# Norm factors of a decoder layer: the sum of squares as the moving operand of a constant, and a reciprocal root with one Newton step

## The chip, the cores and the metric

The kernel runs on one core of a Trainium2 chip. The metric is the device time of one execution, in microseconds (us). Engines are named as the profile names them: PE is TensorE (PEld its weight loads), DVE is VectorE, ACT is ScalarE, POOL is GpSimd, SP is SyncE, which here only issues DMAs. F32R and F32 are two types under which a float32 operand is handed to TensorE.

## What is computed

One layer of a hybrid decoder trunk over 512 tokens and a model width of D = 1024, batch 1, all in float32: a half-step SwiGLU FFN (hidden width 2816), a token mixer (RG-LRU on 512 channels beside sliding-window attention with 8 heads of 64), and a second half-step FFN. Every sub-layer has an RMS norm on its input and one on its output:

```python
def rms_norm(x, g):
    y = xf * lax.rsqrt(jnp.mean(xf * xf, axis=-1, keepdims=True) + RMS_EPS)
    return (y * g).astype(x.dtype)

x = x + 0.5 * rms_norm(swiglu(rms_norm(x, ffn1_pre_g), ffn1_w_gu, ffn1_w_down), ffn1_post_g)
y = concat([rms_norm(y_lru, g_lru_out), rms_norm(y_attn, g_attn_out)]) @ w_o     # mixer, from rms_norm(x, mix_pre_g)
x = x + rms_norm(y, mix_post_g)
x = x + 0.5 * rms_norm(swiglu(rms_norm(x, ffn2_pre_g), ffn2_w_gu, ffn2_w_down), ffn2_post_g)
```

What matters here is the norm factor, 1/sqrt(mean of squares + eps), one number for each token.

## The kernel before

**Layout.** Activations lie transposed: channels on the 128 partitions, the 512 tokens along the free dimension, so a width of 1024 is eight tiles of 128x512. The sum of squares over channels therefore runs over partitions and over tiles. The tiles' squares (ACT, line 552) are added up on DVE or POOL into one 128x512 tile, `acc`; what is left is a sum over the 128 partitions, and the factor is then needed on all partitions, as a 128x512 tile that multiplies the data.

**Matmuls.** Each float32 operand is split into a high part (F32R) and the rest, a low part, and each product is three matmuls: high by high, high by low, low by high. ACT makes a high part by copying (`act.copy`, lines 195 to 215; `x_high`, line 641), DVE or POOL the low part by subtracting it (`x_low`, line 644). Weights come from HBM through `class Weights`: `load` issues the DMA, `round` makes the high part on ACT, `fill(n)` makes both parts until n units beyond those taken are ready. A unit's low part is made by DVE, by POOL, or, for the unit marked `shared`, half by DVE and half by POOL.

**The factor before.** `InvRmsRows` makes it for all 512 tokens at once, `InvRms` for half of them (256). In `stats`, `acc` stands as weights, 128 tokens at a time, and a single column of 1/D moves past it: the means arrive with tokens on partitions, one column per block of 128 tokens (lines 569 and 608). Then follow a square root on ACT (575, 615), a reciprocal on DVE (577, 616), the split into high and low part (583, 584, 617, 618), and a multiplication of the identity matrix by the factors, which gives diagonal blocks (588, 621). In `spread`, a matmul of an all-ones matrix by these diagonals (595, 625) brings the factors to all partitions, in PSUM. In the half-width form the first half has a single plain F32 diagonal, the second a high and a low one. A full-width factor is then copied to SBUF as `R` by ACT (689), or read from PSUM (`lru`, line 1976); a half-width factor is read from PSUM by DVE in `Residual.scale`.

**Where factors are made**, in order of time: `x`, for the first norm (full width; its squares are summed by ACT, so it has no statistics matmul); `r1`, two halves, the norm behind the first FFN; `mx`, full width, before the mixer; `lru`, full width, inside it; `r2`, two halves, behind the mixer; `f2` (shown as `nf`), full width, before the second FFN. Two half-width pairs and three full-width factors thus go the whole way from `acc`. The attention's own norm and the one at the very end are made otherwise and are not touched.

**The boundary.** `boundary` joins a sub-layer to the next one, once as "a" (FFN 1 to mixer: `r1`, then `mx`) and once as "m" (mixer to FFN 2: `r2`, then `f2`). All engines run in an order written out by hand (`manual_schedule`): each executes its instructions in the order in which the code emits them, waits on semaphores, and passes nothing that waits. The last three output chunks, c = 5, 6, 7, are multiplied in two token halves, each product over n = 6 ("a") or n = 8 ("m") tiles of the contraction, three 256-column matmuls for each. The code then goes on as follows, where (k, h) is chunk k of token half h:

- first half of the three products; after each, DVE takes it out of PSUM (751 or 755), ACT squares it, DVE adds it to `acc2` (764 to 768), and `W.fill` prepares weights;
- second half: in the middle of product c = 6 the hook `stats` for half 0, and one contraction tile later `W.fill(4)`; ahead of product c = 7 `spread` of half 0 and the steps for chunks 0 and 1;
- a step for chunk k is: `scale`, DVE multiplies y by the gain and the factor in one instruction (772); `add`, the residual sum into `xT`, on DVE for even k and on POOL for odd k (776); `high`, ACT makes the high part for the next matmul (641);
- `k_high` on PE (540, 541): pass k multiplies chunk k's high part by four weight tiles, each high and low, 8 matmuls; passes 0 to 3 of half 0, then `stats` of half 1, passes 4 and 5, `spread` of half 1, passes 6 and 7, then the eight passes of half 1. Meanwhile the steps of the remaining chunks of half 0 and of all of half 1 run;
- `low` for all chunks (DVE, 644), `W.fill(2)`, the next norm's squares into its `acc` (ACT 552, DVE 681), and `k_low` on PE (547), 32 matmuls of 512 columns. The next full-width factor is asked for in the middle of the product that follows.

In "a" the weight unit that `W.fill(4)` prepares is the `shared` one (DVE and POOL, 195); in "m" its low part is made by POOL alone (215).

Of the kernel before, what the change touches and what calls it, by code (L numbers as in the profile page):

```python
# [8 lines left out]
F32 = mybir.dt.float32  # L9
F32R = mybir.dt.float32r  # L10
# [112 lines left out]
def tile_layer(ctx: ExitStack, tc: tile.TileContext, out: bass.AP, **ins: bass.AP):  # L123
# [357 lines left out]
    ones = const.tile([P, P], F32R, name="ones")  # L481
    dve.memset(ones.bitcast(F32), 1.0)
# [8 lines left out]
    mean_d = filled("mean_d", 1, 1.0 / D)  # L491
    mean_c = filled("mean_c", 1, 1.0 / C)
# [63 lines left out]

    class InvRms:


        def __init__(self, accs, mean, half, name, eps=eps):  # L560
            self.accs, self.mean, self.half, self.name, self.eps = accs, mean, half, name, eps

        def stats(self):
            self.ps = ps = bank(f"rms_{self.name}")
            self.dg = []
            for i in range(2):
                b = 2 * self.half + i
                for j, a in enumerate(self.accs):
                    pe.matmul(ps[:, i:i + 1], a[:, b * P:(b + 1) * P], self.mean, start=j == 0, stop=j == len(self.accs) - 1)
            self.invert(ps[:, :2])  # L570

        def invert(self, ms, scale=1.0):
            n = self.name
            rms = small.tile([P, 2], F32, tag="rms", name=f"rms_s{n}")
            act.activation(rms, ms, AF.Sqrt, bias=self.eps, scale=scale)
            rs = small.tile([P, 2], F32, tag="rs", name=f"rs_{n}")
            dve.reciprocal(rs, rms)
            split = self.half == 1
            factors, w = [rs], ones.bitcast(F32)
            if split:  # L580
                high = small.tile([P, NB], F32R, tag="rh4", name=f"rh4_{n}", bufs=1)[:, :2]
                low = small.tile([P, NB], F32, tag="rl4", name=f"rl4_{n}", bufs=1)[:, :2]
                dve.tensor_copy(high, rs)
                dve.tensor_sub(low, rs, high.bitcast(F32))
                factors, w = [rs, low], ones
            t = wt(f"dg_{n}", T, F32R if split else F32)
            for sl, r in zip(HALF, factors):
                dve.tensor_tensor(t[:, sl].rearrange("p (a b) -> p a b", a=2), ident.unsqueeze(1).to_broadcast([P, 2, P]),
                                  r.unsqueeze(2).to_broadcast([P, 2, P]), op=ALU.mult)
                self.dg.append((w, t[:, sl]))  # L590

        def spread(self):
            o = self.ps[:, T // 2:]
            for i, (w, d) in enumerate(self.dg):
                pe.matmul(o, w, d, start=i == 0, stop=i == len(self.dg) - 1)
            return o


    class InvRmsRows:


        def __init__(self, acc, mean, name):
            self.acc, self.mean, self.name = acc, mean, name

        def stats(self):
            self.ps = ps = bank(f"rms_{self.name}")
            for b in range(NB):
                pe.matmul(ps[:, b:b + 1], self.acc[:, b * P:(b + 1) * P], self.mean, start=True, stop=True)
            self.invert(ps[:, :NB])

        def invert(self, ms, scale=1.0):
            n = self.name
            rms, rs, low = (small.tile([P, NB], F32, tag=t, name=f"{t}_{n}", bufs=1) for t in ("rms4", "rs4", "rl4"))
            high = small.tile([P, NB], F32R, tag="rh4", name=f"rh4_{n}", bufs=1)
            act.activation(rms, ms, AF.Sqrt, bias=eps, scale=scale)
            dve.reciprocal(rs, rms)
            dve.tensor_copy(high, rs)
            dve.tensor_sub(low, rs, high.bitcast(F32))
            self.dg = [wt(f"d{i}_{n}", T, F32R) for i in "hl"]
            for d, r in zip(self.dg, (rs, low)):  # L620
                dve.tensor_tensor(v4(d), ident.unsqueeze(1).to_broadcast([P, NB, P]), r.unsqueeze(2).to_broadcast([P, NB, P]), op=ALU.mult)

        def spread(self):
            for i, d in enumerate(self.dg):
                pe.matmul(self.ps, ones, d, start=i == 0, stop=i == 1)
            return self.ps
# [31 lines left out]
    class Next:  # L658


        def __init__(self, name, pre=None, gain=None):
            self.name, self.pre = name, pre
            self.gain = gain or (lambda c: col(pre, c))
            self.t = {}
            self.xs = x_parts(name)
            self.acc = tmp.tile([P, T], F32, tag="acc", name=f"acc_n{name}", bufs=3)
            self.rms = InvRmsRows(self.acc, mean_d, f"n{name}")
            self.R = None
# [14 lines left out]
        def stats(self):  # L683
            self.rms.stats()
# [1517 lines left out]
```

## Time and profile before

| | us |
|---|---|
| median of 3 runs (lowest to highest) | 835.47 (835.04 to 835.94) |
| the profiled execution's own time | 834.93 |
| its span, first to last instruction | 833.0 |
| PE busy | 825.3 |
| DVE busy | 737.6 |
| ACT busy | 518.5 |
| POOL busy | 164.7 |
| granted TensorE clock, mean | 0.999 |

The profile is one execution. Busy is the time in which an engine had an instruction running; consecutive matmuls overlap, so what a matmul costs is read from the distance between starts. In a timeline row the first number is the start from the beginning of the span, the second the time it took, then engine, line, operation, output and inputs; "x4" is a number of merged instructions, and a bracket at the end tells how long the engine had been idle and what ended that.

### The profile page before, as it was taken

How to read it: one execution, taken by the hardware profiler on the slowest of the kernel's cores; microseconds unless marked ns; L12 is line 12 of the kernel's file. 1: busy time of each engine (PE TensorE's matmuls, PEld its weight loads, DVE VectorE, ACT ScalarE, POOL GpSimd, SP SyncE). 2: the span in 40 equal slices, each digit the busy share in tenths (PEclk: the TensorE clock that was granted, in tenths of full speed). 3: DMA queues.
4: the chain of work that ended last, by engine and by line, in shares of the span. 5: the costliest groups of instructions: out<-in, count | busy, mean ns of one | idle time of the engine just before them, and what ended most of it. 6: DMA issues, size and time to landing. Idle time of an engine off the chain costs nothing.

```text
span 833.0 us, 11751 instructions
## 1 busy us (share of the span) xinstructions
PE 825.3 (99%) x4188; PEld 700.3 (84%) x4188; DVE 737.6 (89%) x1033; ACT 518.5 (62%) x811; POOL 164.7 (20%) x187
## 2 busy tenths in 40 slices
PE   9999999999999999999999999999999999999997
PEld 8888888888888898987888899888888888888885
DVE  5989799998989978888989689998999798898996
ACT  6746656676666654546797446545757677676552
POOL 2022000140320325414531052002005023032001
PEclk9999999999999999999999999999999999999999
DMA  7376408398595897522611140567439949669742
GB/s 254 103 278 226 152 22 322 75 263 253 139 260 170 196 272 243 175 89 82 174 37 51 51 143 10 123 180 253 130 107 239 309 94 252 234 159 260 300 141 102
DMA packets 121835, 144.22 MB, mean 173 GB/s; under 512 B 24168, under 2 KB 76720, under 8 KB 121264
## 3 DMA queue, kind: packets, MB, share of 16 engines
q1 hardware_dynamic: 107280, 112.26, 42.1%
q0 software_dynamic: 13792, 30.42, 16.6%
q10 hardware_dynamic: 704, 0.79, 0.3%
q8 instruction: 33, 0.54, 0.3%
q14 instruction: 26, 0.21, 0.1%
HBM read 100.45 MB, written 39.32 MB: 168 GB/s over the span
## 4 chain that ended last, share of the span: by engine, by line
PE 98%; DVE 0%; DMA 0%; issue 0%; SPq 0%; DVEq 0%
PE ab L1026 10%; PE aa L1026 10%; PE db L1026 5%; PE da L1026 5%; PE yaa L1427 3%; PE a_first L1289 3%; PE bb L1026 3%; PE ba L1026 3%; PE ya L1427 3%; PE yda L1427 2%; PE aa L956 1%; PE yab L2042 1%; PE yab L2041 1%; PE yab L2040 1%; PE wo L1966 1%; PE gt L522 1%
## 5 line engine op out<-in xcount | busy, mean ns | idle before, releaser
L1198 POOL DMA_DIRECT2D yr_a<-stage x36 | 31.1, 1004 | 176.0 <-ACT stage L1195 153.6
L1198 POOL DMA_DIRECT2D yp_b<-stage x42 | 36.5, 1064 | 146.3 <-ACT stage L1195 119.8
L2056 POOL DMA_DIRECT2D yp_b<-stage x8 | 4.4, 547 | 64.7 <-ACT stage L2055 64.3
L745 POOL TENSOR_TENSOR acca_r<-acca_r,sq_r 128x512 f32<-128x512 f32 x6 | 9.1, 1517 | 38.2 <-ACT sq_r L552 38.1
L540 PE MATMUL an<-xh_mx,whi_xl 128*128 128x256 f32 x64 | 15.7, 285 | 0.0
L541 PE MATMUL an<-xh_mx,wlo_xl 128*128 128x256 f32 x64 | 15.5, 283 | 0.0
L2157 ACT ACTIVATE ysq<-yp 128x512 f32<-128x512 f32 (+1 forms) x8 | 4.8, 606 | 16.8 <-DVE yp L2150 16.8
L2160 POOL TENSOR_TENSOR last<-yp,grow 128x512 f32<-128x512 f32 x3 | 3.9, 1288 | 57.0 <-DVE yp L2150 57.0
L522 PE MATMUL gt<-xh_mx,whi_gt 128*128 128x512 f32 x32 | 14.2, 443 | 0.0
L1464 POOL DMA_DIRECT2D yp_a<-zy x16 | 8.7, 555 | 25.5 <-DMA rows_a<-yr_a 17.3
L498 ACT ACT_TABLE_LOAD x9 | 11.5, 1283 | 2.4 <-issue 2.3
L522 PE MATMUL pq<-xh_mx,whi_q 128*128 128x512 f32 x32 | 12.8, 399 | 0.0
L524 PE MATMUL gt<-xh_mx,wlo_gt 128*128 128x512 f32 x32 | 12.6, 394 | 0.0
L522 PE MATMUL pgb<-xh_f,whi_bg 128*128 128x512 f32 x32 | 12.6, 393 | 0.0
L523 PE MATMUL gt<-xl_mx,whi_gt 128*128 128x512 f32 x32 | 12.5, 391 | 0.0
L524 PE MATMUL pq<-xh_mx,wlo_q 128*128 128x512 f32 x32 | 12.5, 390 | 0.0
L523 PE MATMUL pq<-xl_mx,whi_q 128*128 128x512 f32 x32 | 12.5, 390 | 0.0
L524 PE MATMUL pgb<-xh_f,wlo_bg 128*128 128x512 f32 x32 | 12.5, 390 | 0.0
L522 PE MATMUL pub<-xh_f,whi_bu 128*128 128x512 f32 x32 | 12.5, 389 | 0.0
L523 PE MATMUL pub<-xl_f,whi_bu 128*128 128x512 f32 x32 | 12.5, 389 | 0.0
L523 PE MATMUL pgb<-xl_f,whi_bg 128*128 128x512 f32 x32 | 12.5, 389 | 0.0
L524 PE MATMUL pub<-xh_f,wlo_bu 128*128 128x512 f32 x32 | 12.5, 389 | 0.0
(2028 smaller groups left out, 3398.6 us busy)
## 6 DMA issues: line engine op xcount, KB each, us to landing
yp_b<-stage POOLq DMA_DIRECT2D x50, 256.0 KB, 9.1
yr_a<-stage POOLq DMA_DIRECT2D x44, 256.0 KB, 9.9
h_a<-za SPq DMA_DIRECT2D x16, 256.0 KB
h_b<-zb SPq DMA_DIRECT2D x16, 256.0 KB
hxb<-h_b SPq DMA_DIRECT2D x16, 256.0 KB
hxa<-h_a SPq DMA_DIRECT2D x6, 512.0 KB
raw_ad<-in_ffn_w_down SPq DMA_DIRECT2D x2, 1024.0 KB
xT_hbm<-xT POOLq DMA_DIRECT2D x2, 1024.0 KB, 6.1
```

The lines of the kernel that those rows point to most:

```text
L498: act.activation(dummy, eps, func)
L522: pe.matmul(ps, hi[:, k, :], xh, start=start, stop=False)
L523: pe.matmul(ps, hi[:, k, :], xl, start=False, stop=False)
L524: pe.matmul(ps, lo[:, k, :], xh, start=False, stop=stop)
L540: pe.matmul(ps[:, sl], hi[:, k, :], xh, start=k == 0 and not goes_on, stop=False, skip_group_check=True)
L541: pe.matmul(ps[:, sl], lo[:, k, :], xh, start=False, stop=False, skip_group_check=True)
L745: eng.tensor_add(acc, acc, square(part, ALL, f"{self.name}{c}"))
L1026: pe.matmul(b[tb], x[:, blk], w[:, k, :], start=first and q + k + j == 0, stop=q + k == 2 and j == 2, skip_group_check=True)
L1198: pool.dma_start(o, st, accum_op=ALU.add)
L1289: pe.matmul(banks[j][:, sl], ws[j][part][:, k, :], n1.xs[k][xpart][:, sl], start=k == 0 and part == xpart, stop=stop and k == KD - 1)
L1427: pe.matmul(o, x[:, blk], a[:, k, :], start=start and j == 0, stop=stop and j == 2, skip_group_check=True)
L1464: (pool if q % 2 else sync).dma_start(chunks[32 * q:32 * (q + 1), :, i * P:(i + 1) * P], turned[32 * i:32 * (i + 1), :, q])
```

## The change

A constant matrix of -1.0, `minus`, takes the place of `ones` and stands as weights; `acc` is now what moves, as plain F32, in one matmul of 512 or 256 columns. Its output is minus the sum of squares, on all 128 partitions at once. ACT makes an approximate factor r from it with `Abs_reciprocal_sqrt` (its scale turns the sign and divides by D, its bias adds eps) and then a scaled square of r; DVE makes one Newton step in two instructions, the first of them reading the sum from PSUM. The result r lies in SBUF. The statistics matmuls with one column, the roots, the reciprocals, the splits, the diagonals, `spread` and the copy to `R` are gone for these factors. `x` keeps its old way, with `minus` as weights and a sign turned by the copy.

In `boundary`, `stats` of half 0 is asked for one contraction tile earlier (`n // 2 - 1`). In "a", `W.fill(4)` is replaced at its place by a `round` of one unit (ACT only), and comes after the steps for chunks 0 and 1; in "m" it keeps its place. `scale` reads r, in SBUF, where it read the factor in PSUM. The function that ACT preloads is `Abs_reciprocal_sqrt` instead of `Sqrt` in two places.

```diff
-    ones = const.tile([P, P], F32R, name="ones")
-    dve.memset(ones.bitcast(F32), 1.0)
+    minus = const.tile([P, P], F32R, name="minus")
+    dve.memset(minus.bitcast(F32), -1.0)
...
+    NEWTON = {D: (eps4, -1.0 / 256, 1.0 / 16, 3.0), C: (eps, -1.0 / 512, 1.0 / 32, 1.5)}
+
     class InvRms:
-        def stats(self):
-            self.ps = ps = bank(f"rms_{self.name}")
...
-        def spread(self):
...
+        def stats(self, r, sl=slice(0, T), q=None):
+            bias, scale, root, k = NEWTON[self.n]
+            ps = bank(f"rms_{self.name}")[:, sl]
+            pe.matmul(ps, minus.bitcast(F32), self.acc[:, sl], start=True, stop=True)
+            q = wt(f"q_{self.name}")[:, sl] if q is None else q
+            act.activation(r, ps, AF.Abs_reciprocal_sqrt, bias=bias, scale=scale)
+            act.activation(q, r, AF.Square, scale=root)
+            dve.scalar_tensor_tensor(q, ps, self.n * EPS, q, op0=ALU.subtract, op1=ALU.mult)
+            dve.scalar_tensor_tensor(r, q, k, r, op0=ALU.add, op1=ALU.mult)
+            self.r = r
+
+    class InvRmsHalf(InvRms):
...
         def stats(self):
+            t = wt(f"r_{self.name}")
+            super().stats(t[:, HALF[0]], HALF[self.half], t[:, HALF[1]])
...
         def spread(self):
             if self.R is None:
-                self.R = big.tile([P, T], F32, tag="R", name=f"R_{self.name}")
-                act.copy(self.R, self.rms.spread())
+                self.R = self.rms.r
...
-        def spread_a():
-            spread(0)
-            steps((0, 1), 0, bcs[0])
+        def round_next():
+            if W.rounded == W.split:
+                W.round()
+
+        def first_steps():
+            steps((0, 1), 0, res.rms[0].r)
+            W.fill(4)
 
         n = len(xs)
-        hooks = [{}, {n // 2: res.rms[0].stats, n // 2 + 1: lambda: W.fill(4)}, {0: spread_a}]
+        hooks = [{}, {n // 2 - 1: res.rms[0].stats, n // 2 + 1: round_next if parts else lambda: W.fill(4)}, {0: first_steps}]
...
-                preload(AF.Sqrt)
+                preload(AF.Abs_reciprocal_sqrt)
...
     def spread_lru():
-        bc = lrms.spread()
+        bc = lrms.r
...
-            wo_attn([c], lrms.stats)
+            wo_attn([c], lambda: lrms.stats(wt("r_lru")))
```

More of the change, by code (lines that the diff above doesn't have):

```diff
@@ L572, in invert @@
[L572 to L590, printed above, removed]
@@ L592, in spread @@
-        def spread(self):
[L593 to L603, printed above, removed]
-        def stats(self):
[L606 to L626, printed above, removed]
@@ new lines, in __init__ @@
+        def __init__(self, acc, n, name):
+            self.acc, self.n, self.name = acc, n, name
+        def stats(self, r, sl=slice(0, T), q=None):
[8 more added lines that the diff above has]
+            self.r = r
@@ L629, in stream, with __init__ @@
+    class InvRmsHalf(InvRms):
+        def __init__(self, acc, half, name):
+            super().__init__(acc, D, name)
+            self.half = half
+        def stats(self):
+            t = wt(f"r_{self.name}")
+            super().stats(t[:, HALF[0]], HALF[self.half], t[:, HALF[1]])
     def stream():
@@ L666, in __init__ @@
             self.acc = tmp.tile([P, T], F32, tag="acc", name=f"acc_n{name}", bufs=3)
-            self.rms = InvRmsRows(self.acc, mean_d, f"n{name}")
+            self.rms = InvRms(self.acc, D, f"n{name}")
             self.R = None
@@ L730, in __init__ @@
             self.acc, self.acc2 = (tmp.tile([P, T], F32, tag="acc", name=f"acc{i}_{name}", bufs=3) for i in "ab")
-            self.rms = [InvRms([self.acc2], mean_d, h, f"{name}{h}") for h in range(2)]
+            self.rms = [InvRmsHalf(self.acc2, h, f"{name}{h}") for h in range(2)]
         def chunk(self, c, ps, part=None, eng=pool, first=None):
@@ L809, in boundary @@
                 for k in (2, 3):
-                    res.scale(k, 0, bcs[0])
+                    res.scale(k, 0, res.rms[0].r)
                 res.add(2, 0)
@@ L831, in boundary @@
         for k in (6, 7):
-            res.scale(k, 0, bcs[0])
+            res.scale(k, 0, res.rms[0].r)
         for k in (6, 7):
@@ L840, in boundary @@
         k_high(ws, banks, nxt.xs, HALF[0], range(4, 6))
-        spread(1)
         for k in (0, 1):
-            res.scale(k, 1, bcs[1])
+            res.scale(k, 1, res.rms[1].r)
             res.add(k, 1)
@@ L846, in boundary @@
         for k in range(2, KD, 2):
-            steps((k, k + 1), 1, bcs[1])
+            steps((k, k + 1), 1, res.rms[1].r)
         k_high(ws, banks, nxt.xs, HALF[0], range(6, 8))
@@ L1256, in first_lo, with stats @@
         eng.tensor_sub(lo, raw, hi.bitcast(F32))
-    class InvRmsX(InvRmsRows):
+    class InvRmsX:
         def early(self):
-            ss = small.tile([P, NB], F32, tag="ss", name=f"ss_{self.name}", bufs=1)
+            ss, rms, rs, low = (small.tile([P, NB], F32, tag=t, name=f"{t}_x", bufs=1) for t in ("ss", "rms4", "rs4", "rl4"))
+            high = small.tile([P, NB], F32R, tag="rh4", name="rh4_x", bufs=1)
             sx = ssx.rearrange("p (b h) -> p b h", h=2)
             dve.tensor_add(ss, sx[:, :, 0], sx[:, :, 1])
-            self.invert(ss, 1.0 / D)
-        def stats(self):
-            self.ps = bank(f"rms_{self.name}")
-    n1.rms = InvRmsX(None, None, "x")
+            act.activation(rms, ss, AF.Sqrt, bias=eps, scale=1.0 / D)
+            dve.reciprocal(rs, rms)
+            dve.tensor_copy(high, rs)
+            dve.tensor_sub(low, rs, high.bitcast(F32))
+            self.dg = [wt(f"d{i}_x", T, F32R) for i in "hl"]
+            for d, r in zip(self.dg, (rs, low)):
+                dve.tensor_tensor(v4(d), ident.unsqueeze(1).to_broadcast([P, NB, P]), r.unsqueeze(2).to_broadcast([P, NB, P]), op=ALU.mult)
+        def stats(self, r):
+            ps = bank("rms_x")
+            for i, d in enumerate(self.dg):
+                pe.matmul(ps, minus, d, start=i == 0, stop=i == 1)
+            act.activation(r, ps, AF.Copy, scale=-1.0)
+            self.r = r
+    n1.rms = InvRmsX()
     warm = bank("warm")
@@ L1276, in spin @@
         for i in range(n):
-            pe.matmul(warm[:, (i % 4) * P:(i % 4 + 1) * P], ones.bitcast(F32), ones.bitcast(F32), start=True, stop=True)
+            pe.matmul(warm[:, (i % 4) * P:(i % 4 + 1) * P], minus.bitcast(F32), minus.bitcast(F32), start=True, stop=True)
     spin(WARM)
@@ L1954, in tile_layer @@
     W.round()
-    preload(AF.Sqrt)
-    lrms = InvRmsRows(accl, mean_c, "lru")
+    preload(AF.Abs_reciprocal_sqrt)
+    lrms = InvRms(accl, C, "lru")
     res = Residual("r2", lambda c: col("mix_post_g", c))
```

19 lines of the change are left out of this document (3 added, 16 removed).

## The prediction

> **What bounds the kernel now.** I read the page's first part, its chain of work, and the waits of PE.
>
> ```profile
> span 833.0 us, 11751 instructions
> ...
> PE 825.3 (99%) x4188; PEld 700.3 (84%) x4188; DVE 737.6 (89%) x1033; ACT 518.5 (62%) x811; POOL 164.7 (20%) x187
> ...
> PE 98%; DVE 0%; DMA 0%; issue 0%; SPq 0%; DVEq 0%
> ```
>
> PE is busy for 825.3 of 833.0 us and is 98% of the chain that ends last. Its column of issued matmuls is the kernel's length, so the change counts in two ways only: PE work it adds or removes, and gaps it opens or closes in that column. The boundaries are where gaps can open: there PE multiplies what DVE, POOL and ACT have finished just before. One gap is already visible, in boundary "a", pass 1 of half 1:
>
> ```profile
> 349.75 0.28 PE L541 MATMUL an<-xh_mx,wlo_xl 128*128 128x256 f32 x1
> 349.96 0.39 PE L540 MATMUL an<-xh_mx,whi_xl 128*128 128x256 f32 x1
> ```
>
> Starts stand 0.12 us apart here, but 0.21 at this place. The chain that makes high parts has no reserve there, and a later factor lengthens the kernel one for one.
>
> **PE's own work.** First a half-width factor of boundary "a", half 0, then the full-width `mx`, both from PE's timeline.
>
> ```profile
> 336.31 0.50 PE L569 MATMUL rms_r<-mean_d,accb_r 128*128 128x1 f32 x4
> 336.68 0.36 PE L522 MATMUL ay<-hha,whi_ad 128*128 128x256 f32 x1
> 336.88 0.28 PE L523 MATMUL ay<-hla,whi_ad 128*128 128x256 f32 x1
> ...
> 337.71 0.28 PE L524 MATMUL ay<-hha,wlo_ad 128*128 128x256 f32 x1
> 337.92 0.67 PE L595 MATMUL rms_r<-dg_r,ones 128*128 128x256 f32 x2
> 338.24 0.47 PE L522 MATMUL ay<-hha,whi_ad 128*128 128x256 f32 x1
> 338.55 0.28 PE L523 MATMUL ay<-hla,whi_ad 128*128 128x256 f32 x1
> ```
>
> The statistics cost 0.37 (336.31 to 336.68) and 0.08 more at the next step (0.20 instead of 0.12): 0.45. From 337.71 to 338.55 there would be 0.24 without the spread; it costs 0.60, of which 0.09 is its late start (337.92, not 337.83). So a plain F32 matmul of 256 columns takes 0.51, about four steps of 0.12, and its result is complete 0.67 after its start.
>
> ```profile
> 366.77 0.95 PE L608 MATMUL rms_nmx<-mean_d,acc_nmx 128*128 128x1 f32 x8
> 367.58 0.49 PE L522 MATMUL pk<-xh_mx,whi_kv 128*128 128x512 f32 x1
> 367.91 0.40 PE L523 MATMUL pk<-xl_mx,whi_kv 128*128 128x512 f32 x1
> ...
> 370.46 0.39 PE L625 MATMUL rms_nmx<-dh_nmx,ones 128*128 128x512 f32 x1
> 370.69 0.39 PE L625 MATMUL rms_nmx<-dl_nmx,ones 128*128 128x512 f32 x1
> 370.91 0.40 PE L522 MATMUL pv<-xh_mx,whi_kv 128*128 128x512 f32 x1
> ```
>
> Full width: statistics 0.81 + 0.10 (0.33 instead of 0.23), spread 0.45, together 1.36. The new matmul moves 512 columns as plain F32, which no row shows. Bounds: two steps of 0.23 (0.46) below, twice the 0.51 (1.02) above; I take 0.93, four steps and the same small rest, nearest to the 256-column row. Three factors (`mx`, `lru`, `f2`) save 3 x (1.36 - 0.93) = **1.3 us** (1.0 to 2.7). Half width: half 0 saves 0.45 + 0.60 - 0.51 = 0.54, half 1 (spread in two F32R matmuls, about 0.23) 0.45 + 0.23 - 0.51 = 0.17; both boundaries 1.4 us, if nothing else waits. `x` keeps its matmuls: 0.
>
> **The chain from sum to factor**, half 0 of "a". Durations from the groups by line:
>
> ```profile
> L1582 ACT ACTIVATE r<-rg,cols 128x512 f32<-128x512 f32 x4 | 2.7, 687 | 3.1 <-PE rg L1580 3.1
> L552 ACT ACTIVATE sq_nmx<-xT 128x512 f32<-128x512 f32 x7 | 3.7, 619 | 0.0
> L552 ACT ACTIVATE sq_r<-yp_a 128x256 f32<-128x256 f32 x6 | 2.5, 418 | 7.0 <-DVE yp_a L751 7.0
> ```
>
> The new root reads PSUM with a bias from a tile, as L1582 does at 512 columns (0.69); 256 columns fewer are worth 0.20, so 0.48 (bounds 0.42 and 0.69). The square takes 0.42, each Newton instruction 0.48, like the 256-column scales below; a hand-over takes 0.04. The statistics start one contraction tile earlier, at 336.31 - 0.36 = 335.95, and are complete at 336.62; root 336.66 to 337.14, square to 337.59, Newton 337.63 to 338.61. Before, the spread was complete at 337.92 + 0.67 = 338.59. The factor is no earlier. DVE then still has chunk 6 to take out of PSUM (it did that at 338.29), so the first scale starts at 338.87 instead of 338.63, and the 0.5 us that PE saved is spent waiting for chunk 0.
>
> **What moves: scale now reads two SBUF tiles.** This decides. Below DVE and POOL around half 0 of "a", then of "m".
>
> ```profile
> 337.69 0.69 DVE L195 TENSOR_TENSOR wlo_xl<-raw_xl__3135,whi_xl 128x512 fp32r<-128x512 f32 x1
> 338.29 0.42 DVE L751 TENSOR_TENSOR yp_a<-ay,yp_a 128x256 f32<-128x256 f32 x1
> 338.63 0.87 DVE L772 SCALAR_TENSOR_TENSOR yp_a<-yp_a,half_g,rms_r 128x256 f32<-128x256 f32 x2
> 339.42 0.42 DVE L776 TENSOR_TENSOR xT<-yp_a,xT 128x256 f32<-128x256 f32 x1
> 339.76 0.86 DVE L772 SCALAR_TENSOR_TENSOR yp_a<-yp_a,half_g,rms_r 128x256 f32<-128x256 f32 x2
> ...
> 340.88 0.96 DVE L768 TENSOR_TENSOR accb_r<-accb_r,sq_r 128x256 f32<-128x256 f32 x1
> ```
>
> ```profile
> 338.22 1.31 POOL L195 TENSOR_TENSOR wlo_xl<-raw_xl__3135,whi_xl 128x512 fp32r<-128x512 f32 x1 [7.91 <-ACT whi_xl L210]
> 339.58 0.85 POOL L776 TENSOR_TENSOR xT<-yp_a,xT 128x256 f32<-128x256 f32 x1
> 340.70 0.85 POOL L776 TENSOR_TENSOR xT<-yp_a,xT 128x256 f32<-128x256 f32 x1 [0.27 <-DVE yp_a L772]
> ```
>
> ```profile
> 493.56 2.40 POOL L215 TENSOR_TENSOR wlo_bu<-raw_bu__4802,whi_bu 128x1024 fp32r<-128x1024 f32 x1 [2.45 <-ACT whi_bu L210]
> ```
>
> ```profile
> 494.25 0.87 DVE L772 SCALAR_TENSOR_TENSOR y_r<-y_r,cols,rms_r 128x256 f32<-128x256 f32 x2
> 495.04 1.20 DVE L776 TENSOR_TENSOR xT<-y_r,xT 128x256 f32<-128x256 f32 x1
> ```
>
> The scales (y in SBUF, factor in PSUM) run undisturbed inside a POOL instruction: two in 0.87 in the midst of POOL's 2.40, two in 0.86 beside 339.58. The instructions with both inputs in SBUF don't: the add of 495.04 takes 1.20 instead of 0.42 and ends at 496.24, 0.28 after POOL's 495.96; the one of 340.88 takes 0.96 and ends 0.29 after POOL's 341.55. So DVE with two SBUF inputs waits for POOL's instruction, and needs 0.28 after it. In the new kernel all 32 half-width scales are of that kind.
>
> [...]
>
> Placing DVE's, POOL's, ACT's and PE's instructions in the written order, with these durations and this wait:
>
> - "a", half 0. Chunk 0's high part is ready at 340.62 (it was 340.38), pass 0 starts 0.10 later than before (its row is below). `W.fill(4)` now stands behind chunk 0 and 1: DVE's half of the shared unit waits for POOL's add (339.82 to 340.67) and ends at 341.22; POOL's half, 1.31 long, follows until 342.38; the scale of chunk 2, queued behind on DVE, ends at 342.66 instead of 340.2. High part 2 is ready at 343.94, pass 2 was due at 342.6: PE waits 1.4. High part 3 stands on ACT behind the square of chunk 7, whose sum stands on DVE behind one more wait for POOL: ready at 345.55, 0.65 more. Passes 2 to 5 thus run **2.2 us** late.
> - "a", half 1: the 0.5 us of two root instructions ahead of high parts 6 and 7, and each pair of scales waits once for POOL's add; pass 1 starts 2.6 late instead of 349.96, and the rest follows from PE alone. **+2.6 us** in all, PE's own saving included.
> - "m": the copy that POOL's 2.40 us need stands on ACT behind root and square, so POOL has it from 494.21 to 496.61. The scale of chunk 0, at 494.46, ends at 496.89 instead of 494.7; pass 0 starts 1.2 late, pass 3 1.6, and pass 1 of half 1 2.0. **+2.0 us.**
>
> ```profile
> 339.87 1.63 ACT L641 ACTIVATE xh_mx<-xT,cols 128x256 fp32r<-128x256 f32 x3 [0.65 <-DVE xT L776]
> ...
> 340.57 0.28 PE L540 MATMUL an<-xh_mx,whi_xl 128*128 128x256 f32 x1
> ```
>
> DVE ends its low parts 3.9 us later in "a" while PE is 2.6 later. The next `acc` hides that: its last two adds,
>
> ```profile
> 363.82 1.49 DVE L681 TENSOR_TENSOR acc_nmx<-acc_nmx,sq_nmx 128x512 f32<-128x512 f32 x2
> ```
>
> end at 365.31, 1.46 ahead of PE's 366.77; 0.15 of that cover is left, and without it every further tenth on DVE is PE's too. Sum: 2.6 + 2.0 - 1.3 = **+3.3 us**, span 836.3. The profiled execution took 834.93 around its span of 833.0, the median of the runs is 835.47; I add the sum to the median: 838.8.
>
> [...] The rows show no gain from SBUF instead of PSUM as a source: the add out of PSUM at 338.29 and that of two SBUF tiles at 339.42 both take 0.42. [...] I go by the row.
>
> **Rivals.**
> - *The scales don't wait* (the stored factor is read like PSUM was). For it: nothing in the rows; against it: every two-SBUF instruction above that met POOL. Then "a" is +0.3 and "m" +0.1 by the same placing, since the factor still comes no earlier: 0.4 - 1.3 = -0.9, 834.6.
> - *PE's saving is the whole effect*, the chain being quicker than my rows say. Place: the two passes 1 of half 1. Price: -1.3 - 1.4 = -2.7, 832.8. It decides once the factor is about 0.5 us earlier at each half than placed above and POOL hides behind other work. For it: DVE loses the diagonals, reciprocals and splits. Against it: the gap at 349.96.
> - *The new function's table lacks Square or Copy.* A load takes 1283 ns:
>
> ```profile
> L498 ACT ACT_TABLE_LOAD x9 | 11.5, 1283 | 2.4 <-issue 2.3
> ```
>
> Two more in each of four half-width chains: 8 x 1.28 = +10, some 849. Squares and copies run behind the loaded root now without another load; whether the new function's set holds them no row tells.
>
> **How the numbers follow.** Waits for POOL: 0.60; scales don't wait: 0.20; PE's saving whole: 0.17; tables: 0.03. A change of under 0.2% (1.7 us) can hardly be told from none. The first and last are slower: 0.63; the second is the same: 0.20; the third faster: 0.17. The likeliest gives 838.8; its own range is 837.2 to 840.5: a root of 0.42 to 0.69 moves it by -0.3 to +0.9, the 512-column matmul by -1.4 to +0.3, POOL's exact turn by about 0.5 either way. For 8 in 10 I go down over 834.6 to 833.8, and leave out 832.8 and the tables.
>
> **What would show it.** Right: scales (L772's successor) with a mean well over 474 ns, some near 1.5 us; those of chunk 2 in "a" and chunk 0 in "m" ending 0.28 after a POOL instruction; PE gaps before passes 2 and 3 in "a" and pass 0 in "m"; `mx`, `lru`, `f2` costing PE 0.93 each. Wrong: scales all at 474 ns, passes on time, more than 9 table loads on the preload's line, or a 256-column root far under 0.42.

## The result, and the profile after

The changed kernel takes 843.97 us (median of 5 runs, 842.82 to 844.64); the kernel before, measured beside it, 835.51 (835.04 to 836.17). The ratio is 1.0099, with a 95% interval of 1.0084 to 1.0114: **slower by 1.0%**. The prediction had slower by 0.4%, 838.8, with a range to 840.5. The sign is right, and the time lies 3.5 us outside the range.

The profiled execution took 844.64, the slowest of the five. From its page: the span, PE's busy time, the first DMA queue, and the engines' shares of the chain that ended last.

```profile
span 842.6 us, 11651 instructions
...
PE 827.8 (98%) x4148; PEld 697.0 (83%) x4148; DVE 742.3 (88%) x1016; ACT 519.6 (62%) x816; POOL 165.9 (20%) x187
...
q1 hardware_dynamic: 107280, 112.26, 43.2%
...
PE 83%; DVE 9%; ACT 3%; issue 2%; DMA 2%; POOL 0%; SPq 0%; DVEq 0%; ACTq 0%
```

PE has 40 matmuls fewer, yet its share of the chain fell from 98% to 83%: PE now waits in places. And the first DMA queue, with the same packets and the same bytes as before, has 43.2% of the engines' time instead of 42.1%, over a longer span. The view of what PE waited for names the places (us in total, times, longest):

```profile
PE an L538 <- ACT xh_mx L599: 2.0, 4, 1.1
PE vt L1629 <- DVE vT L1518: 1.8, 1, 1.8
PE mn L538 <- ACT xh_f L599: 1.5, 2, 1.3
...
PE ydb L2008 <- DVE hla L864: 1.1, 1, 1.1
PE ab L981 <- ACT bb L986: 0.3, 1, 0.3
```

The first and third lines are the two boundaries, which the prediction expected. The transposes `vt`, inside the mixer, and the last rows, in FFN 2, it didn't.

Since PE's column of matmuls is the kernel's length, the loss can be laid out along it. For each matmul that both kernels have, I took its start in the other kernel minus its start before; a stretch's number below is how much that difference grew in it (us). "to 10" is the first 10 us, which scatter (-0.14 to +1.48 in the column); "to 330" is the rest of FFN 1; "a" and "m" are the boundaries, "mx", "lru", "f2" the three full-width factors, "to 395" the stretch behind `mx` up to 395 us of the kernel before, "rest" all behind `f2`. The table also holds the profiled executions of the ten experiments, which the next section takes one by one.

```
                     to 10  to 330       a      mx  to 395  to 440     lru       m      f2    rest     end
after                -0.13   +0.63   +2.23   -0.52   +3.40   +0.06   -0.22   +1.70   -0.53   +2.95   +9.56
halves_only          +0.12   +0.03   +2.23   -0.03   +0.00   +0.00   -0.02   +1.79   +0.02   +0.00   +4.15
full_only            -0.05   +0.07   -0.01   -0.55   +3.51   +0.04   -0.18   -0.01   -0.57   -0.00   +2.26
r_in_psum            +1.48   +0.70   +1.30   -0.52   +3.45   +0.00   -0.22   +0.48   -0.53   +1.55   +7.70
vt_ahead             -0.02   +1.45   +2.23   -0.52   -0.04   +1.65   -0.23   +1.69   -0.53   +2.71   +8.38
aligned              +0.23   -0.11   +2.23   -0.54   +3.49   +0.08   -0.22   +1.69   -0.57   +0.00   +6.28
before_shifted       +0.41   +0.89   -0.01   -0.00   -0.00   -0.03   +0.01   +0.00   +0.01   +0.78   +2.05
all_mended           +0.24   -0.02   +1.31   -0.55   +1.20   +0.59   -0.22   +0.47   -0.57   +0.00   +2.46
full_new_order       -0.02   +0.02   +0.00   -0.55   +1.20   +0.57   -0.23   -0.01   -0.57   +0.00   +0.42
full_second_order    -0.14   +0.00   -0.01   -0.55   -0.05   +0.33   -0.19   -0.01   -0.57   -0.00   -1.18
all_second_order     +0.37   +0.00   +1.11   -0.55   -0.05   +0.34   -0.19   +0.46   -0.57   +0.00   +0.93
```

The first row, grouped: boundaries 2.23 + 1.70 = 3.93 (forecast 4.6); three factors -1.27 (forecast -1.3); behind `mx` 3.40 + 0.06 = 3.46 (forecast 0); FFN 1 and FFN 2 0.63 + 2.95 = 3.58 (forecast 0); the first 10 us -0.13. The terms of the sum held, but two places that it did not contain lost 7.0 us. The experiments ask what they are.

**The boundaries.** The groups of the scales and of the residual adds of "m" on DVE (busy us, mean ns):

```profile
L729 DVE SCALAR_TENSOR_TENSOR y_r<-y_r,cols,r_r 128x256 f32<-128x256 f32 x16 | 11.5, 751 | 0.0
...
L729 DVE SCALAR_TENSOR_TENSOR yp_a<-yp_a,half_g,r_r 128x256 f32<-128x256 f32 x16 | 10.0, 661 | 0.0
...
L733 DVE TENSOR_TENSOR xT<-y_r,xT 128x256 f32<-128x256 f32 x8 | 3.3, 415 | 0.0
```

The scales have a mean of 751 and 661 ns where they had 473 and 474. The means hide two kinds. Of the 32 scales 21 take 471 to 481 ns, as before. The other 11 take 0.94 to 2.49 us; each of them began while a POOL instruction ran and ended 0.28 or 0.29 us after it. Two scales that began before POOL's instruction took 0.48, and that instruction, an add, 0.92 where it otherwise takes 0.84: the one that comes second waits. In "a", DVE and then POOL around the scales of chunks 2 and 3, and the PE passes that waited:

```profile
340.35 1.22 DVE L195 TENSOR_TENSOR wlo_xl<-raw_xl__3131,whi_xl 128x512 fp32r<-128x512 f32 x1
341.49 1.91 DVE L729 SCALAR_TENSOR_TENSOR yp_a<-yp_a,half_g,r_r 128x256 f32<-128x256 f32 x2
```

```profile
340.98 1.74 POOL L195 TENSOR_TENSOR wlo_xl<-raw_xl__3131,whi_xl 128x512 fp32r<-128x512 f32 x1
```

```profile
344.33 0.39 PE L538 MATMUL an<-xh_mx,whi_xl 128*128 128x256 f32 x1 [1.13 <-ACT xh_mx L599]
```

Two scales that took 0.87 before take 1.91. The first of them stands across POOL's instruction, which ends at 340.98 + 1.74 = 342.72, and ends itself at 343.00. PE's pass 2 waits 1.13 us for chunk 2. The prediction had it as a wait of 1.4.

**Behind mx.** First DVE in the kernel before, then in the changed one, from the stretch in which the factor `R` arrives to `vT`:

```profile
369.75 1.22 DVE L215 TENSOR_TENSOR wlo_q<-raw_q,whi_q 128x1024 fp32r<-128x1024 f32 x1
370.89 0.42 DVE L1418 CAST up<-upf 128x512 uint8<-128x512 f32 x1
...
371.73 1.30 DVE L1560 TENSOR_TENSOR xp<-an,R_mx 128x512 f32<-128x512 f32 x2 [0.41 <-ACT R_mx L689]
...
382.06 0.68 DVE L1552 TENSOR_TENSOR vT<-pv,R_mx 128x512 f32<-128x512 f32 x1
```

```profile
371.94 0.69 DVE L570 SCALAR_TENSOR_TENSOR q_nmx<-rms_nmx,q_nmx 128x512 f32<-128x512 f32 x1 [1.47 <-ACT q_nmx L569]
372.67 0.69 DVE L571 SCALAR_TENSOR_TENSOR R_mx<-q_nmx,R_mx 128x512 f32<-128x512 f32 x1
373.28 1.22 DVE L215 TENSOR_TENSOR wlo_q<-raw_q,whi_q 128x1024 fp32r<-128x1024 f32 x1
374.41 1.52 DVE L1384 CAST up<-upf 128x512 uint8<-128x512 f32 x1
375.86 0.68 DVE L1526 TENSOR_TENSOR xp<-an,R_mx 128x512 f32<-128x512 f32 x1
...
386.17 0.68 DVE L1518 TENSOR_TENSOR vT<-pv,R_mx 128x512 f32<-128x512 f32 x1
```

Before, `R` went by way of PE and ACT, and while it did, DVE made a low part (`wlo_q`) and the cast `up`; it then waited 0.41 us for `R`. Now DVE itself makes `R`, and the low part and the cast stand behind that, ahead of `xp`. The cast takes 1.52 instead of 0.42: POOL's subtraction for the gates runs beside it, from 373.45 to 375.65, and the cast ends 0.28 after that. `xp` starts 4.13 us later (375.86 against 371.73) and `vT` 4.11, where PE is 2.2 later by the table's first four columns (-0.13 + 0.63 + 2.23 - 0.52). Of the remaining 1.9 us the cast's extra 1.10 is the larger part. PE waits 1.84 us for `vT`, and this happens to its clock (windows; behind the five engines' busy times stands the granted clock):

```profile
386.00:388.00 2.00, 1.10 (x5) 1.10 (x6) 1.45 (x3) 2.00 (x4) 2.00 (x1) 0.70 0.00 0
388.00:390.00 2.00, 2.00 (x7) 1.52 (x6) 2.00 (x3) 1.98 (x4) 0.87 (x2) 0.50 0.00 0
390.00:392.00 2.00, 2.00 (x10) 1.67 (x9) 2.00 (x2) 1.99 (x3) 0.88 (x1) 0.95 0.00 0
```

The clock's record has 0.5 from 386.80 to 390.21, 3.41 us; it begins 0.10 before the first `vt`, at the end of the wait. In that stretch 512-column matmuls start 0.43 apart instead of 0.23.

### The profile page after: what moved, and what is told of

Read it like the earlier page. It is cut to its first block, busy times and chain, and to the rows that moved or that the text cites. A ratio compares the mean times of both kernels' runs of the same rounds, so it can differ in the third digit from the quotient of the medians.

```text
span 842.6 us, 11651 instructions
## 1 busy us (share of the span) xinstructions
PE 827.8 (98%) x4148; PEld 697.0 (83%) x4148; DVE 742.3 (88%) x1016; ACT 519.6 (62%) x816; POOL 165.9 (20%) x187
## 3 DMA queue, kind: packets, MB, share of 16 engines
q1 hardware_dynamic: 107280, 112.26, 43.2%
## 4 chain that ended last, share of the span: by engine, by line
PE 83%; DVE 9%; ACT 3%; issue 2%; DMA 2%; POOL 0%; SPq 0%; DVEq 0%; ACTq 0%
PE aa L981 10%; PE ab L981 9%; PE da L981 5%; PE db L981 4%; PE yaa L1393 3%; PE a_first L1255 3%; PE bb L981 3%; PE ya L1393 3%; PE ba L981 3%; PE yda L1393 2%; DMA rows_a<-yr_a 1%; PE yab L2006 1%; PE yab L2007 1%; PE yab L2008 1%; PE yea L1393 1%
## 5 line engine op out<-in xcount | busy, mean ns | idle before, releaser
L538 PEld LDWEIGHTS an<-xh_mx,whi_xl 128*128 128x128 f32 x64 | 12.2, 191 | 3.1 <-ACT xh_mx L599 3.0
L856 ACT CAST hhs<-s4b 128x512 fp32r<-128x512 f32 x4 | 2.5, 622 | 18.0 <-DVE s4b L893 18.0
L599 ACT ACTIVATE xh_f<-xT,cols 128x256 fp32r<-128x256 f32 x16 | 8.0, 507 | 7.8 <-DVE xT L733 6.4
L599 ACT ACTIVATE xh_mx<-xT,cols 128x256 fp32r<-128x256 f32 x16 | 8.0, 506 | 7.5 <-DVE xT L733 6.1
```

Source lines behind the costliest of these rows:

```text
L538: pe.matmul(ps[:, sl], hi[:, k, :], xh, start=k == 0 and not goes_on, stop=False, skip_group_check=True)
L599: act.activation(x[0][:, sl], src, AF.Copy, scale=gain)
```

## The experiments

Each kernel was timed in five rounds beside the kernel before; four, four and two ran together, each group on one chip. The kernel before had medians of 835.18, 835.03 and 835.23 in the three. The code below is abridged to the lines that matter.

### One half of the change alone: halves_only and full_only

`halves_only` keeps the new way for `r1` and `r2` and the boundary's new order, and takes the old way for `mx`, `lru`, `f2`; `full_only` the other way round.

```diff
 # halves_only                                   # full_only
-self.rms = InvRms(self.acc, D, f"n{name}")      # (boundary and half-width class as before)
+self.rms = InvRmsRows(self.acc, mean_d, f"n{name}")
-lrms = InvRms(accl, C, "lru")
+lrms = InvRmsRows(accl, mean_c, "lru")
 # in the class that goes back, in both, against the kernel before (`minus` spreads, hence the -1.0):
-act.activation(rms, ms, AF.Sqrt, ...)
-dve.reciprocal(rs, rms)
+act.activation(rms, ms, AF.Abs_reciprocal_sqrt, ...)
+dve.tensor_scalar(rs, rms, -1.0, None, op0=ALU.mult)
```

> Only the half-width factors r1 and r2 are made the new way, with the boundary's new order; mx, lru and f2 go back to columns, diagonals and spread. So that no table load is added, their root is Abs_reciprocal_sqrt and a multiplication by -1 stands where the reciprocal stood: the Newton step is left out of these three, and their factors are approximate. Theory (boundaries +4.0, full-width factors -1.3 on PE and +3.4 by DVE's queue behind mx): 835.5 + 4.0 = 839.5 if the rest of the loss is this run-to-run scatter, up to 840.5. Rival (DVE's 1.3 us of extra lateness from boundary a is what makes vT late, whatever the mx factor is): the vt wait stays in part and the time is 841 to 843.

> Only the full-width factors mx, lru and f2 are made the new way; r1 and r2, and the boundary's order, are as before the change, with Abs_reciprocal_sqrt and a multiplication by -1 where Sqrt and the reciprocal stood (no Newton step in these two, so their factors are approximate). Theory (three factors save 1.3 us of PE; Newton instructions ahead of wlo_q on DVE make vT late): 835.5 - 1.3 = 834.2 for PE alone, and up to +3.4 if vT is late without boundary a's part, 837.6. Rival (the 3.4 us need both, the later DVE from boundary a and the Newton instructions): 834.2 to 834.8.

Measured: `halves_only` 839.25 (839.00 to 839.91), ratio 1.005 [1.0038, 1.0062]. `full_only` 837.44 (835.35 to 838.32, 11 runs), ratio 1.0024 [1.0016, 1.0033]. What PE waited for, first in `halves_only`, then in `full_only`:

```profile
PE an L540 <- ACT xh_mx L630: 2.0, 4, 1.1
PE mn L540 <- ACT xh_f L630: 1.5, 2, 1.3
```

```profile
PE vt L1664 <- DVE vT L1553: 1.9, 1, 1.9
```

Each half of the change loses in its own places. The half-width factors lose 4.1 us, in the two boundaries and nowhere else; the full-width ones lose 2.3, which is -1.3 on PE and +3.5 behind `mx`. The rivals of both fall: `vT` is in time when only the boundaries are late, and late when only `mx` is made the new way. Of `full_only`'s eleven runs nine had a mean clock of 0.996 and took 837.05 or more; the two with 0.998 took 835.35 and 836.32. `aligned`, below, is alike: 840.02 to 840.17 at a mean clock of 0.999, 841.20 and 841.54 at 0.997. So, by the mean clocks, the drop comes in some executions and not in others, and is worth 1 to 2 us of the 3.5. A trace with the wait and without the drop was not taken.

But 4.1 + 2.3 = 6.4, and the whole change loses 8.5. In the table, both kernels have nothing in "rest", where the changed kernel has 2.95, and next to nothing in "to 330", where it has 0.63. That was open now.

### r in PSUM: r_in_psum

```diff
-ps = bank(f"rms_{self.name}")[:, sl]
+rms = bank(f"rms_{self.name}")
+ps = rms[:, sl]
+out = r if to is None else rms[:, to]    # to: the other half, for half-width factors
 ...
-dve.scalar_tensor_tensor(r, q, k, r, op0=ALU.add, op1=ALU.mult)
+dve.scalar_tensor_tensor(out, q, k, r, op0=ALU.add, op1=ALU.mult)
```

> The changed kernel, with one thing different: the last Newton instruction of the half-width factors writes r into the unused half of their PSUM bank, so each of the 32 half-width scales has one SBUF input again. Theory (scales with two SBUF inputs wait for POOL): the L729 scales return to some 475 ns, the two boundaries give back nearly all of their 4.0 us (2.2 in a, 1.8 in m) and keep the 0.4 that the prediction's placing without the wait gives, so the time is 844.0 - 3.6 = 840.4. [...]

Measured: 842.08 (839.84 to 843.62), ratio 1.008 [1.0068, 1.0092]. From its groups:

```profile
L731 DVE SCALAR_TENSOR_TENSOR yp_a<-yp_a,half_g,rms_r 128x256 f32<-128x256 f32 x16 | 7.0, 474 | 0.0
L731 DVE SCALAR_TENSOR_TENSOR y_r<-y_r,cols,rms_r 128x256 f32<-128x256 f32 x16 | 7.0, 473 | 0.0
L735 DVE TENSOR_TENSOR xT<-y_r,xT 128x256 f32<-128x256 f32 x8 | 4.6, 579 | 0.0
```

The theory is confirmed: with one operand moved to PSUM and nothing else changed, the scales are back at 474 and 473 ns from 661 and 751. Had the boundaries been late only because the new chain is longer and `W.fill(4)` stands later, the scales would have stayed where they were. The price was too high: the boundaries give back 2.1 us (2.23 to 1.30, 1.70 to 0.48), not 3.6. Part of the wait falls on the next instruction with two SBUF inputs, the residual adds: those of "m" go from 415 to 579 ns. In the kernel before they had 515:

```profile
L776 DVE TENSOR_TENSOR xT<-y_r,xT 128x256 f32<-128x256 f32 x8 | 4.1, 515 | 0.0
```

There too one add waited for POOL, the 1.20 at 495.04; in the changed kernel the scale ahead of it waits in its place (2.49), and here the add waits again, for 1.71. `all_mended` below repeats the boundaries' losses, with 1.31 and 0.47.

### vT ahead of a low part: vt_ahead

```diff
-pv = in_product("pv")
+pv = in_product("pv", (), 0)          # fills nothing ahead
 vT = scaled(wt("vT"), pv)
+W.fill(AHEAD, True)
```

> The changed kernel, with one DVE instruction moved: vT (the multiplication of pv by R) stands ahead of the subtraction wlo_q that waits for ACT's whi_q, not behind it; ACT's and PE's orders are unchanged. Theory (PE waited 1.84 us for vT and its clock was then granted at half for 3.4 us; DVE's queue behind the mx factor is the cause): vT is ready some 3 us earlier, the wait before the transposes and the stretch at a clock of 0.5 are both gone, and the time is 844.0 - 3.4 = 840.6. Rival (the low clock came from elsewhere and only the wait itself goes): 844.0 - 1.8 = 842.2. Rival (DVE's lateness only moves to the next consumer, wlo_q for pq1 or the copy of vt): 843.5 to 844.

Measured: 843.66 (843.44 to 844.32), ratio 1.0104 [1.009, 1.0119]: no faster. PE's waits tell why:

```profile
PE ya L520 <- ACT hha L918: 0.9, 1, 0.9
PE rg L1546 <- POOL xcl L1569: 0.8, 1, 0.8
PE cur L1715 <- DVE home L1599: 0.3, 1, 0.3
```

The wait before `vt` and the half clock are both gone (3.40 to -0.04 in the table; the granted clock is 1.00 in each window from 384 to 392). That the wait brings the drop fits all twelve traces: the four with this wait (the changed kernel, `full_only`, `r_in_psum`, `aligned`) have 3.41 us at 0.5, the other eight stay at 1.00 until their last few us. But DVE is as late as it was, and the next consumers, the gates' matmuls `rg` and the scores `cur`, now cost PE 1.65. That is the second rival, for about half of the 3.44 that the stretch gained. FFN 1 takes 0.82 more, 1.45 instead of 0.63, where `ya` waits for `hha`. So the trace ends 1.2 us earlier than the changed kernel's, which was the slowest of its five; the medians differ by 0.3, within their intervals.

### The addresses: aligned and before_shifted

What do `halves_only` and `full_only` share that the three kernels with a loss in "rest" lack? They need the columns `mean_d` and `mean_c`. The change deletes these two constants, and each takes 32 bytes of a partition's SBUF. By the addresses in the built programs, most large tiles behind the constants begin at multiples of 2,048 bytes in the kernel before (`raw` at 139,264, a `stage` tile at 49,152), and 64 bytes lower in the changed kernel (139,200; 49,088). The packets of the traces, grouped by their size:

```
mean time of a packet, ns     512 B (26,696)   1,024 B (25,856)   2,048 B (41,856)
before                              30.3              51.3              114.6
after                               38.0              51.4              115.6
halves_only                         30.2              51.0              114.6
full_only                           30.3              51.0              114.7
r_in_psum                           38.0              51.6              116.3
vt_ahead                            37.9              51.7              115.9
aligned                             30.2              50.8              114.5
before_shifted                      38.0              51.8              115.5
```

The groups mix directions. Between 110 and 260 us all 6,144 packets of 512 bytes in the first queue are stores out of SBUF (`h_a<-za`), and they go from 31.7 ns to 41.5. Before 60 us all 3,912 are loads into SBUF, and they go from 27.0 to 30.3. Of the 2,048-byte packets those of the first queue stay (95.2, then 94.5); those of GpSimd's queue, mainly stores of `stage`, go from 176.7 to 182.9. So it is mainly the way out of SBUF that became slower.

Two kernels test it: the changed one with the room kept, and the one before with its tiles moved.

```diff
 # aligned: the changed kernel
+spare0, spare1 = (filled(f"spare{i}", 1, 0.0) for i in range(2))
 # before_shifted: the kernel before
+spare0 = filled("spare0", 112, 0.0)
```

> The changed kernel with two unused one-column constants where mean_d and mean_c stood, so that every tile behind them lies again at the SBUF address that it had before the change; without them all of these tiles lie 64 bytes lower, off the multiples of 512. Theory (512-byte DMA packets take 38.0 ns in the kernels with the lowered tiles and 30.3 in the others; transfers land later, and FFN 2 and the end of FFN 1 wait for them): the packets go back to 30 ns, the steps at the rows_a reads and behind 740 us go, and the time is 844.0 - 2.9 = 841.1, near the sum of the two partial kernels, 835.2 + 4.1 + 2.2 = 841.5. Rival (these steps come from the boundaries and the mx factor together, or are scatter): 844.0 within 0.5.

> The kernel before the change with one unused constant of 448 bytes, so that the tiles behind it lie 64 bytes below a multiple of 512, as in the changed kernel; nothing else differs. Theory (the address costs DMA time, and that reaches PE): 512-byte packets 38 ns, the first queue's share of DMA time 43% instead of 42%, and the time 0.7 to 3.0 above before, 836 to 838.2. Rival (the address costs DMA time that this kernel hides): packets 38 ns, time 835.2 within 0.5. Rival (the address is not the cause): packets 30 ns.

Measured: `aligned` 840.17 (840.02 to 841.54), ratio 1.0067 [1.0054, 1.0079]; `before_shifted` 837.58 (836.62 to 840.10), ratio 1.0036 [1.0022, 1.0049]. The kernel before, slowed by 0.36% through the address alone. From its page, and from its waits:

```profile
span 835.1 us, 11752 instructions
...
q1 hardware_dynamic: 107280, 112.26, 43.5%
```

```profile
DVE raw_ax__1941 L296 <- DMA raw_ay__2124<-in_ffn_w_gu: 4.1, 1, 4.1
...
DVE zy L1456 <- DMA rows_a<-yr_a: 2.4, 1, 2.4
...
PE ya L523 <- ACT hha L964: 0.4, 1, 0.4
PE ydb L2043 <- DVE hla L910: 0.3, 1, 0.3
```

DVE waits 4.1 us for a weight transfer, and 2.4 for `rows_a`. The longest such waits in the kernel before:

```profile
DVE zy L1455 <- DMA rows_a<-yr_a: 1.6, 1, 1.6
...
DVE raw_ax__1440 L296 <- DMA raw_ay__1623<-in_ffn_w_gu: 0.7, 1, 0.7
```

So transfers land later, hold up DVE, and PE then waits at `ya`, as in `vt_ahead`, and at `ydb`, as in the changed kernel. Followed through the two traces, the 4.1 us is not what reaches `ya`: DVE is 4.4 us late at 230 us and has made up all but 0.4 at 255. It is the wait for `rows_a`, which makes DVE 0.8 later at 301 us, and ACT's `hha` 1.0. In FFN 2 three weight transfers cost DVE 3.7 us each, which it makes up only in part: it is some 2.8 late when PE needs `hla`. In `aligned` both waits of PE are gone, DVE's longest wait for a weight transfer is 1.0, and "rest" is 0.00. So the third cause is the deletion of two columns that are no longer read. It is worth 1.67 us in the profiled `before_shifted` (0.89 + 0.78), 3.58 in the profiled changed kernel, and 0.3% between the ratios of `aligned` and the changed kernel, some 2.7 us. A part of these 2.7 is the clock: by the mean clocks the changed kernel's median execution (0.997) had the drop, that of `aligned` (0.999) had not. Executions of like clock, each set against the kernel before beside it, differ by 2.1 to 2.3.

### All three mended, and the full-width half alone in another order

`all_mended` joins `aligned` and `r_in_psum` with another order behind `mx`. `full_new_order` has the boundaries and half-width factors exactly as before the change, the full-width ones new, and the same order; its roots' tables (`Sqrt` and `Abs_reciprocal_sqrt`) are loaded ahead.

```diff
 pk = in_product("pk", {4: mx.stats}, 2)
-W.fill(3)
 mx.spread()
 neg, upf = masks()                     # without its cast on DVE
 split_gates()
 R = mx.R
 xps = [conv_in(ci, b) for ci, b in enumerate(xl_banks)]
+dve.tensor_copy(up8f, upf)
 ...
-pv = in_product("pv")
+pv = in_product("pv", (), 0)
 vT = scaled(wt("vT"), pv)
+W.fill(2)
```

> The changed kernel with the three suspected causes taken away at once: the two constants' room kept (addresses as before), r of the half-width factors in PSUM, and the order behind mx changed so that pq1's and pq2's low parts and the cast up stand behind xp, or vT, on DVE. Theory (the causes add): 844.0 - 2.9 (addresses) - 2.1 (scales at 475 ns, as the PE steps of the run r_in_psum have it) - 3.4 (vt wait and low clock) = 835.6. Rival (one cause covers another, so that PE meets the next late transfer or queue): 837 to 840.

> The half-width factors and the boundaries exactly as before the change, the full-width ones mx, lru and f2 the new way with their Newton step, the order behind mx changed as in the run all_mended, addresses congruent to those of before, and the roots' tables loaded ahead at three more places. Theory (what the change gains is the three full-width matmuls, and only DVE's queue behind mx stood against it): 835.2 - 1.3 = 833.9, and no stretch at half clock. Rival (DVE is late for the next consumer, or one of the three loads stands in a chain): 834.5 to 837.

Measured: `all_mended` 837.24 (837.10 to 839.20), ratio 1.003 [1.0018, 1.0042]; `full_new_order` 835.21 (834.55 to 835.78, 11 runs), ratio 1.0002 [0.9993, 1.0011]. The rivals are right in both. PE's waits in `full_new_order`:

```profile
PE pq L525 <- DVE wlo_q L215: 0.9, 1, 0.9
PE cur L1751 <- DVE home L1635: 0.3, 1, 0.3
```

The order was overcorrected: the low part for the next projection now stands behind the convolution, and 1.20 + 0.57 us in the table eat what the three factors save. In both kernels the second Newton instruction of `mx` also takes 1.68 us instead of 0.69: it has two SBUF inputs, and POOL's subtraction for the gates now runs beside it (in `full_new_order` from 369.78 to 371.07, the Newton instruction from 369.95). `xp` is still in time in `full_new_order` (371.73, as before the change). The addresses and the scales do add up as expected: `all_mended` has 0.00 in "rest" and 1.31 + 0.47 in the boundaries.

### A second order: full_second_order and all_second_order

```diff
+neg, upf = masks()                           # both ahead of pk, with POOL's part for the gates
+split_gates()
-pk = in_product("pk", {4: mx.stats}, 2)
+pk = in_product("pk", {4: mx.stats}, 3)      # pq1's low part ahead of the root
 ...
 vT = scaled(wt("vT"), pv)
+W.fill(3)
 # all_second_order only, boundary "a":
+round_next()                                 # behind the first halves of the three products
 # the hooks, in words:
-n // 2 - 1: stats, n // 2 + 1: round_next; W.fill(4) behind steps (0, 1)
+n // 2 - 1: W.fill(4), then stats
```

> As full_new_order, with another order behind mx: the masks and the split of the gates stand ahead of the product pk, pq1's low part is made ahead of the mx root (DVE was idle 2.8 us there), and only vT and the cast up stand ahead of pq2's low part. full_new_order lost what it had gained to two waits, 1.06 us for pq2's low part behind the convolution and 0.61 at cur. Theory (the order was overcorrected, nothing else): both go, PE keeps the three savings, 835.0 - 1.3 = 833.7. Rival (DVE is full from the mx factor to cur, so that any order makes PE wait somewhere): 834.5 to 835.5.

> As all_mended (addresses kept, r of the half-width factors in PSUM), with the order behind mx of full_second_order, and in boundary a the shared unit's low parts back ahead of the half-width chain: ACT's cast stands behind the first half of the three products, W.fill(4) just ahead of the statistics of half 0. all_mended kept 1.0 us of a's loss and 0.5 of m's. Theory (a's rest comes from W.fill(4) behind chunk 1: DVE's half of the unit waits 0.8 us for POOL there and the scales of chunks 2 and 3 stand behind it): passes 2 and 3 of a come in time, a falls from +1.0 to between -0.5 and 0, m stays at +0.5, and with -1.3 from the full-width factors the time is 833.7 to 834.2. Rival (a's rest is the length of the new chain): pass 0 and pass 2 stay as late as in all_mended, and the time is 834.8 to 835.3.

Measured: `full_second_order` **834.01** (833.47 to 834.84, 11 runs), ratio 0.9987 [0.9978, 0.9996]: faster than the kernel before, by 1.2 us. Its page, and the one wait of PE that is new:

```profile
span 831.8 us, 11703 instructions
...
PE 823.9 (99%) x4164; PEld 697.6 (84%) x4164; DVE 738.7 (89%) x1025; ACT 525.4 (63%) x818; POOL 164.8 (20%) x187
```

```profile
PE sc L1762 <- ACT sc L1796: 0.3, 1, 0.3
```

The gain is the three matmuls' (-0.55, -0.19, -0.57), less 0.33 at one softmax. The Newton instruction is back at 0.69 and the cast at 0.42. So the full-width half of the change is sound once DVE's queue is ordered for it.

`all_second_order` took 835.99 (835.43 to 838.15, 11 runs), ratio 1.0012 [1.0003, 1.0021], which neither theory had. Passes 2 and 3 of "a" come in time, as the first theory said. But pass 0 now waits 1.5 us, and "a" costs 1.11 instead of 1.31. PE's wait, then DVE and POOL around the shared unit:

```profile
PE an L539 <- ACT xh_mx L602: 1.5, 1, 1.5
```

```profile
337.25 1.30 DVE L724 TENSOR_TENSOR accb_r<-acca_r,sq_r 128x256 f32<-128x256 f32 x1 [1.00 <-ACT sq_r L551]
338.48 0.68 DVE L195 TENSOR_TENSOR wlo_xl<-raw_xl__3135,whi_xl 128x512 fp32r<-128x512 f32 x1
```

```profile
336.98 1.30 POOL L195 TENSOR_TENSOR wlo_xl<-raw_xl__3135,whi_xl 128x512 fp32r<-128x512 f32 x1 [6.55 <-PE rms_r L569]
```

An add of two SBUF tiles takes 1.30 beside it instead of 0.42, and the Newton step stands behind that add and the low part. Wherever the unit was put, it met the half-width chain; a place where it doesn't was not found, and a version with the unit's second half on DVE was not tried.

## Why the prediction was wrong, point by point

- **"The scales read two SBUF tiles, and DVE waits for POOL": right.** Eleven of the 32 scales waited, passes 0, 2 and 3 of "a" and pass 0 of "m" were late, and the wait left the scales when r lay in PSUM. The size: 2.23 and 1.70 against 2.6 and 2.0, PE's saving included.
- **"The next acc hides that; 0.15 of that cover is left": right for `acc`.** Its adds end at 365.21 + 4.13 = 369.34, and the statistics start at 369.50, a plain step of 0.23 behind the matmul ahead of them:

```profile
365.21 4.13 DVE L639 TENSOR_TENSOR acc_nmx<-acc_nmx,sq_nmx 128x512 f32<-128x512 f32 x5
```

```profile
369.27 0.39 PE L522 MATMUL pk<-xh_mx,wlo_kv 128*128 128x512 f32 x1
369.50 1.02 PE L566 MATMUL rms_nmx<-acc_nmx,minus 128*128 128x512 f32 x2
...
370.58 0.39 PE L521 MATMUL pk<-xl_mx,whi_kv 128*128 128x512 f32 x1
```

- **"Three factors save 1.3": right in the sum, in part by luck.** PE has -0.52, -0.22 and -0.53. From 369.27 to 370.58 there would be 0.46 without the new matmul, so it costs 0.85 (I took 0.93), and each factor saves 0.5 where it is made. Behind `lru` 0.3 is lost again, where PE's weight load waits 0.5 us for DVE's `yll` (it was 0.2). Two small errors cancel.
- **The sum: the failed step.** "Sum: 2.6 + 2.0 - 1.3" treats the full-width factors as PE's matter alone. I followed the half-width chain instruction by instruction through DVE's queue, and for `mx` only asked whether `acc` is in time for PE. Behind the factor DVE's queue was not followed: the diagonals leave it and two Newton instructions of 0.69 enter it, but later, and what used to be done while `R` travelled over PE and ACT now stands in front of `R`'s users. The sum had 0 for this place; `full_only` shows that it alone costs 3.5 us: a wait of 1.9 and the stretch at half clock that begins with it. Whoever costs an edit at nothing should name the work that hides it; here that was the round trip, and the change removes it.
- **The deleted constants: not in the working at all.** The diff shows two lines go, `mean_d` and `mean_c`, and I counted them as nothing. They shift every tile allocated behind them by 64 bytes. `before_shifted` prices this at 0.36% without any other part of the change.
- **The rivals.** "The scales don't wait" was wrong on its premise. It also had "a" at +0.3 and "m" at +0.1 in that case; `r_in_psum`, where they don't wait, has 1.30 and 0.48, where the adds and the shared unit's low part still do. Of "PE's saving is the whole effect" (-1.3 - 1.4) `full_second_order` measures the first part, -1.2; no run shows the second. The table loads stayed at nine.
- **The range** was built from the unknown prices inside the terms I had. Both misses were terms I didn't have, and both of one sign.

## What to carry to other kernels

When a factor stops travelling over other engines and is made by the engine that uses it, list what that engine did during the journey: all of it now stands ahead of the first use. When an operand moves from PSUM to SBUF, look at what GpSimd does beside each instruction that reads it: here the scales' means went from 474 and 473 ns to 661 and 751. Moving it back is one line, but here a part of the wait then fell on the next instruction with two SBUF inputs, the adds of "m", whose mean went from 415 to 579 ns. And when a diff deletes or adds a small tile ahead of large ones, compare the addresses and the time per DMA packet, of one size and one direction (here 31.7 and 41.5 ns for 512-byte stores out of SBUF), before looking for a cause in the schedule.

## What the runs showed of the hardware

- **A tile's address cost DMA time, mainly on the way out of SBUF.** With tiles 64 bytes below a multiple of 512, 512-byte packets took 38.0 ns instead of 30.3 (26,696 of them). The stores out of SBUF took 1.31 times as long (31.7 to 41.5 ns), the loads into SBUF 1.12 times (27.0 to 30.3). At 1,024 bytes, where nearly all packets are loads, they took the same 51 ns. How the address slows the stores, and why the loads of 512 bytes became slower and those of 1,024 didn't, stays open.
- **A gap of 1.84 us went with a halved TensorE clock.** The granted clock fell to 0.5 for 3.41 us, from 0.10 before to 0.77 behind the end of the wait for `vT`, in all four traces that have this wait (1.8 to 1.9 us), and in none of the others before their last few us. Waits of 1.3 us (the changed kernel, "m") and 1.5 (`all_second_order`, "a") brought no drop. By the mean clocks some executions of kernels with the wait had no drop either (two of `full_only`'s eleven at 0.998, the other nine at 0.996). What decides between them, and why the stretch lasts 3.41 us, no run shows.
- **The wait for POOL reached a cast too.** A cast of 128x512 from float32 to uint8, with a single input, took 1.52 us beside a POOL subtraction, ending 0.28 after it, and 0.42 without it. The prediction had this wait only for instructions with two SBUF inputs.
